# Second half of w_out loaded in a row, down-phase factors split earlier on VectorE, last rows' sums reordered

## The chip, the cores and the metric

One core of a Trainium2 chip runs the kernel. The metric is the device time of one execution in microseconds (us). The engines are TensorE (PE, matrix products, with PEld for its weight loads), VectorE (DVE), ScalarE (ACT), GpSimd (POOL) and SyncE (SP, which here only issues transfers). The 16 DMA engines move data between memory and the chip's buffers.

## The reference, cut to what matters

The input has 1024 rows (T) of 1024 columns (D), in float32.

```python
mod = c_act @ w_ada[l] + b_ada[l]
sh1, sc1, g1, sh2, sc2, g2 = [m[:, None, :] for m in jnp.split(mod, N_MOD, axis=-1)]
h = rmsnorm(x, pre_w_mix[l]) * (1.0 + sc1) + sh1
proj = h @ w_in[l]
# windowed attention -> attn (512 columns); gated linear recurrence -> rec (512 columns)
mix = jnp.concatenate([attn, rec], axis=-1) @ w_out[l]
x = x + g1 * rmsnorm(mix, post_w_mix[l])
h2 = rmsnorm(x, pre_w_mlp[l]) * (1.0 + sc2) + sh2
y = jnp.square(jax.nn.relu(h2 @ w_up[l])) @ w_down[l]       # 4096 hidden columns
x = x + g2 * rmsnorm(y, post_w_mlp[l])
```

## The kernel before

Every large product is made of three matmuls: each operand is split into a rounded high part (a copy on ACT) and a low part (raw minus high, on DVE or POOL), and hi*hi, hi*lo and lo*hi are added in one bank of PE's accumulator (PSUM). A "split" below is this pair of passes over one block of 128 x 512. Names end in r (raw), h and l: `wo_1r` is a raw block of the second half of w_out, `wo_1l` its low part.

The stages follow each other: norm and projections, attention, the recurrence heads (`head_proj`, `head_core`), the out projection, the second norm with its transposes, the up phase and the down phase. Instructions of one engine run in the order in which they are written or placed. A scheduler places them by priority; between `pin(True, ...)` and `pin(False, ...)` the named engines keep the written order, and `tc.issue_after(m)` places what is inside behind the instruction m. SP issues nearly all loads, in one queue.

**Out projection.** w_out is split in two halves of 512 columns with eight row blocks each. `load_wo(half)` loads and splits them; odd blocks have their low part made on POOL, even ones on DVE. The raw blocks pass through a ring of three buffers (`raw_`), so a load waits until the split that used its buffer is done. `op_prep` splits the mixed rows, `op_mm` multiplies, `out_proj` normalises, adds x (loaded as `xr`) and stores: rows of blocks 3 and 7 to the scratch tensor `x1d`, the others to the output itself, onto which the end adds. `cr` are the first blocks of w_up (w_u), `a_2` and `a_3` later blocks of it.

**Second norm and up phase.** `second_raw(th)` transposes half th of the rows (four row blocks) for eight column blocks on PE; behind each ACT and DVE make h and its splits (`bt_1h`, `bt_1l` and so on). `up_cl(f, th)` makes the 24 matmuls of one classical product of the up phase into bank `pu`; `rl` is ACT's relu out of that bank. The rest of the up phase and the whole down phase use a Strassen-Winograd scheme with seven products.

**Down phase.** It runs over (group g, product n). Groups have 4, 4, 3, 3 and 2 hidden blocks, products come in the order 1, 5, 6, 3, 7, 2, 4, and each has four row steps t. `dslot` makes the matmuls of one step, then the step's sum is added by DVE (`acc<-pda`, where pda, pdb, pdc are the banks). The factors (`dw` from the weights, `du` from the up phase) are loaded and split ahead by a queue `seq`: `pump(k)` takes the next k entries and splits each with one ACT and one DVE pass; `target(i)` says how far the queue must be by the end of product i. Gate entries in the same queue sum the row of g2 into `gw2`, and `gate_row` spreads it over the partitions by four matmuls and multiplies.

**Last group and last rows.** The last group is written out as a loop over 24 steps ordered by `order`, with a table `later` of things to do some steps on: `square` (ACT), `root` (DVE and POOL, the power -1/2), `gated` (times gw2), `scaled` (ACT) and `onto_x`, an accumulating store issued by POOL. `last_rows` finishes row blocks 3 and 7 by DVE passes that add x and by plain stores.

Of the kernel before, what the change touches and what calls it, by code (L numbers as in the profile page):

```python
# [47 lines left out]
def hybrid_layer(ctx: ExitStack, tc: tile.TileContext, I, out, dbg=None):  # L48
# [734 lines left out]
    def head_proj(h, th, prev=None, hook=None):  # L783
# [42 lines left out]
        DVE.tensor_tensor(sub4(k4), b4[:, :, :, CH - 1:CH].broadcast_to([P, 4, 4, CH]), b4, ALU.subtract)  # L826
# [98 lines left out]

    def load_wo(half, ks=range(KB)):
        for k in ks:
            wo[half].append(load_split(hT_, f"wo{k}_{half}", I["w_o"][k][:, half * 512:half * 512 + 512],
                                       eng=POOL if k % 2 else DVE))
# [66 lines left out]
    load_wo(0)  # L996
    next(cores[6])
# [51 lines left out]
    x1d = dram.tile([2, P, D], F32, tag="x1d", name="x1d")  # L1049
    xn2 = [None] * TB  # L1050

    def out_proj(tb):
# [14 lines left out]
        for half in range(2):  # L1067
# [5 lines left out]
            nc.gpsimd.dma_start(x1d[tb // 4][:, hs] if tb % 4 == 3 else out[tb * P:(tb + 1) * P, hs], xr)  # L1073
# [22 lines left out]
    def second_raw(th):  # L1096
        for kb in range(KB):
# [212 lines left out]
    def entry_gate(half, k):  # L1310
        def use(raw):
            acc = gw2[:, half * 512:half * 512 + 512]
            if k == 0:
                DVE.tensor_scalar(acc, raw, cs[:, 0:1], None, ALU.mult)
            else:
                DVE.scalar_tensor_tensor(acc, raw, cs[:, k:k + 1], acc, ALU.mult, ALU.add)
        seq.append((f"wada5_{half}_{k}", lambda: I["wada"][5, half, k], use))

    gates = [(half, k) for half in range(2) for k in range(KB)]
    for i, (g, n) in enumerate(stages):  # L1320
# [3 lines left out]
        if 11 <= i and gates:  # L1324
            entry_gate(*gates.pop(0))
        ends.append(len(seq))
    for tb in (3, 7):
        for half in range(2):
            seq.append((f"x1_{tb}_{half}", lambda tb=tb, half=half: x1d[tb // 4][:, half * 512:half * 512 + 512], None))
# [32 lines left out]
    def up_cl(f, th):  # L1362
        pst = mm_ps(f"pu{f}_{th}")
# [8 lines left out]
    for f in range(3):  # L1372
        up_cl(f, 0)
    pin(True, ACT, DVE, POOL)
    second_raw(1)
    pin(False, ACT, DVE, POOL)
    x2ctx.close()
    gw2 = const.tile([P, D], F32, tag="gw1", name="gw2")
    uctx = ExitStack()
# [7 lines left out]
    for f in range(4):  # L1387
        up_cl(f, 1)
# [152 lines left out]
    def target(i):  # L1541

        j = i
        while j + 1 < len(stages) and j + 1 - i <= (2 if i < 14 else 4) and \
                sum(len(GROUPS[stages[m][0]]) for m in range(i, j + 2)) <= 15:
# [5 lines left out]
    def gate_row(t):  # L1551

        hs = [slice(half * 512, half * 512 + 512) for half in range(2)]
        for half in range(2):
            if t == 0:
                hi, lo = split(gw2[:, hs[half]], lambda name, dt: hT_(name, dt), f"g5{half}")
                b5, w5 = hT_(f"b5{half}"), hT_(f"w5{half}")
                nc.gpsimd.dma_start(b5, I["b_g2"][hs[half]].partition_broadcast(P))
                nc.gpsimd.dma_start(w5, I["postw2"][hs[half]].partition_broadcast(P))
                g5[half] = hi, lo, b5, w5  # L1560
            elif t == 2:
                hi, lo, b5, w5 = g5[half]
# [3 lines left out]
            elif t == 3:  # L1566
                DVE.tensor_tensor(gw2[:, hs[half]], g5["p", half], g5[half][2], ALU.add)
                DVE.scalar_tensor_tensor(gw2[:, hs[half]], gw2[:, hs[half]], float(D ** 0.5), g5[half][3], ALU.mult, ALU.mult)
# [9 lines left out]
    for i, (g, n) in enumerate(stages[:28]):  # L1578
        goal = max(prev, target(i))
        for t in range(4):  # L1580
# [7 lines left out]
            want = prev + (goal - prev) * (t + 1) // 4  # L1588
# [3 lines left out]
            if i == 27:  # L1592
# [19 lines left out]
    def gated(tb, half, eng=POOL):  # L1612
        eng.tensor_tensor(accs[tb][half], accs[tb][half], gw2[:, half * 512:half * 512 + 512], ALU.mult)
# [13 lines left out]
    def onto_x(tb):  # L1627

        for half in range(2):
# [4 lines left out]
    order += [(21, 3, 0), (23, 3, 1), (25, 3, 2)]  # L1634
    order.sort()
    bk = {}
    for step, (_, t, k) in enumerate(order):
# [11 lines left out]
        if step < 6:  # L1649
            pump(2)  # L1650
        if k >= 3 and t < 3:
# [4 lines left out]
            else:  # L1656
                on(step + 2, lambda tb=tb: root(tb))
                on(step + 2, lambda tb=tb, half=half: gated(tb, half, DVE))
# [10 lines left out]
    def last_rows():  # L1669
# [5 lines left out]
        gl = [m_(f"gl{half}") for half in range(2)]  # L1675

# [21 lines left out]
        dmm(bx[:, 256:512], g, 4, t, True, slice(256, 512))  # L1698
# [88 lines left out]
```

## Time and profile before

| what | us |
|---|---|
| median of 3 runs | 1112.27 (1111.29, 1113.03, 1112.27) |
| profiled execution | 1115.94 |
| its span in the profile | 1114.2 |
| PE busy | 1082.6 (97%) |
| DVE busy | 811.3 (73%) |
| ACT busy | 592.5 (53%) |
| POOL busy | 394.9 (35%) |
| mean clock of PE in the span | 0.995 |

Times within the profile count from the span's start. The profiled execution took 1.74 us more than its span, and 3.67 us more than the median of the runs, so a sum made from the trace is a difference to be taken off the median, not a time by itself. A matmul is shown busy for longer than the distance to the next, because neighbours overlap in PE. Waits are put down to the instruction that ended them.

### The profile page before, as it was taken

To read this page: it belongs to the slowest core of one execution; us is meant where nothing else is said; L and a number is where in the kernel's file an instruction comes from. 1 tells how busy PE (TensorE), PEld (TensorE's weight loads), DVE (VectorE), ACT (ScalarE), POOL (GpSimd) and SP (SyncE) were. 2 spreads that over 40 slices of the span, in tenths; PEclk is the share of its full clock that TensorE was granted. 3 is DMA by queue.
4 is the path that set the end of the run, shared out by engine and by line. 5 is a ranking of instruction groups with operands and counts; after the bars stand their busy time and mean duration, and the time that the engine had idled before them with its cause. 6 is when DMAs were issued, how large, how long until landed. Compare 5 with 4: busy or idle time off the path is not lost.

```text
span 1114.2 us, 16145 instructions
## 1 busy us (share of the span) xinstructions
PE 1082.6 (97%) x5480; PEld 883.9 (79%) x5480; DVE 811.3 (73%) x1332; ACT 592.5 (53%) x1229; POOL 394.9 (35%) x522
## 2 busy tenths in 40 slices
PE   8899999999999999999999999999999999999995
PEld 7788676778888878888888888888888888888874
DVE  3975877878865673639877767776678787999685
ACT  4645554374565654566655555556565543456334
POOL 2644311034223653422334434444333334300045
PEclk9999999999999999999999999999999999999998
DMA  9701300534410443323577676776899788988546
GB/s 346 257 7 39 133 1 19 194 102 133 134 49 10 130 144 114 112 78 107 199 251 264 222 251 236 250 243 235 274 370 333 269 282 270 335 284 257 165 113 119
DMA packets 101971, 204.16 MB, mean 183 GB/s; under 512 B 13152, under 2 KB 13808, under 8 KB 101888
## 3 DMA queue, kind: packets, MB, share of 16 engines
q1 hardware_dynamic: 86112, 154.78, 40.4%
q0 software_dynamic: 15488, 47.82, 14.3%
q8 instruction: 43, 0.70, 0.3%
q10 hardware_dynamic: 288, 0.52, 0.1%
q14 instruction: 40, 0.33, 0.1%
HBM read 148.03 MB, written 55.05 MB: 182 GB/s over the span
## 4 chain that ended last, share of the span: by engine, by line
PE 77%; DVE 7%; DMA 6%; POOL 3%; ACT 3%; issue 2%; SPq 0%; DVEq 0%; POOLq 0%; ACTq 0%
PE pda L39 13%; PE pua L39 13%; PE pdc L39 7%; PE po L39 7%; PE puc L39 6%; PE pu L39 4%; PE pdb L39 3%; PE pub L39 3%; PE phg L39 3%; PE pv L39 3%; PE phq L39 3%; PE phf L39 2%; PE pq L39 2%; DMA wa<-wada 2%; PE sc L39 1%
## 5 line engine op out<-in xcount | busy, mean ns | idle before, releaser
L39 POOL TENSOR_TENSOR b<-b,b 128x512 f32<-128x512 f32 x64 | 89.5, 1399 | 221.3 <-DMA b<-w_dn 221.0
L39 ACT ACTIVATE s<-s 128x512 f32<-128x512 f32 x84 | 52.9, 631 | 34.0 <-DVE s L39 32.7
L39 ACT ACTIVATE dw<-dwr 128x512 fp32r<-128x512 f32 x72 | 45.3, 629 | 42.4 <-DMA dwr<-td 21.9
L39 DVE TENSOR_TENSOR dw<-dwr,dw 128x512 fp32r<-128x512 f32 x72 | 56.3, 782 | 4.8 <-ACT dw L39 4.8
L39 DVE TENSOR_TENSOR acc<-pda,acc 128x512 f32<-128x512 f32 x68 | 46.1, 682 | 13.5 <-PE pda L39 13.4
L39 POOL DMA_DIRECT2D td<-b x64 | 36.1, 564 | 19.0 <-POOL b L39 19.0
L39 DVE TENSOR_TENSOR wt<-s,wt 128x512 fp32r<-128x512 f32 x42 | 37.1, 884 | 1.4 <-ACT wt L39 1.3
L39 ACT ACTIVATE s<-pua 128x512 f32<-128x512 f32 x28 | 16.7, 596 | 38.2 <-PE pua L39 32.7
L39 ACT ACT_TABLE_LOAD x28 | 35.9, 1283 | 1.2 <-PEq L1780 0.7
L39 POOL DMA_DIRECT2D b<-w_dn x64 | 34.4, 540 | 2.7 <-issue 2.7
L39 DVE TENSOR_TENSOR wt<-a,wt 128x512 fp32r<-128x512 f32 x42 | 34.5, 822 | 0.0
L39 DVE SCALAR_TENSOR_TENSOR macc<-wada,cs,macc 128x512 f32<-128x512 f32 x42 | 32.7, 779 | 2.0 <-DMA wada<-wada 1.3
L39 POOL TENSOR_TENSOR comb<-comb,rd 128x512 f32<-128x512 f32 x8 | 11.7, 1458 | 63.3 <-DVE rd L39 44.2
L39 ACT ACTIVATE wt<-s 128x512 fp32r<-128x512 f32 x42 | 26.3, 627 | 12.3 <-DVE s L39 12.1
L39 PE MATMUL pua<-bt_3h,wt 128*128 128x512 f32 x84 | 32.7, 389 | 0.0
L39 PE MATMUL pua<-bt_0h,wt 128*128 128x512 f32 x84 | 32.7, 389 | 0.0
L39 PE MATMUL pua<-bt_1h,wt 128*128 128x512 f32 x84 | 32.7, 389 | 0.0
L39 PE MATMUL pua<-bt_2h,wt 128*128 128x512 f32 x84 | 32.7, 389 | 0.0
L39 PE MATMUL pda<-dw,du_6h 128*128 128x512 f32 x96 | 29.8, 392 | 1.1 <-DVE acc L39 1.1
L39 DVE TENSOR_TENSOR s<-puc,s 128x512 f32<-128x512 f32 x14 | 9.7, 690 | 28.2 <-issue 27.2
L39 DVE TENSOR_TENSOR acc<-pdc,acc 128x512 f32<-128x512 f32 x36 | 24.5, 682 | 7.5 <-PE pdc L39 7.5
L39 PE MATMUL pdc<-dw,du_3h 128*128 128x512 f32 x96 | 29.7, 390 | 0.2 <-DVE acc L39 0.2
(761 smaller groups left out, 3804.7 us busy)
## 6 DMA issues: line engine op xcount, KB each, us to landing
dur<-ud SPq DMA_DIRECT2D x112, 256.0 KB, 4.2
wada<-wada SPq DMA_DIRECT2D x64, 256.0 KB, 3.5
b<-w_dn POOLq DMA_DIRECT2D x64, 256.0 KB, 5.0
td<-b POOLq DMA_DIRECT2D x64, 256.0 KB, 3.0
dwr<-td SPq DMA_DIRECT2D x64, 256.0 KB, 3.9
a<-w_u SPq DMA_DIRECT2D x56, 256.0 KB, 4.3
dwr<-w_dn SPq DMA_DIRECT2D x48, 256.0 KB, 4.3
ud<-s SPq DMA_DIRECT2D x42, 256.0 KB, 3.6
```

The lines of the kernel that those rows point to most:

```text
L39: ins = op(*args, **kw)
```

## The change

It has five parts. (1) The eight raw blocks of the second half of w_out are loaded in a row on SP, placed behind the last head's instruction `k4`; the first four into tiles of their own, the others into the ring of three. `load_wo(1)` then splits them. (2) The scratch tensor keeps three halves instead of four: half 0 of row block 3 goes to the output, and its final sum is made by an accumulating store of POOL. (3) The second transposes are cut after three of eight blocks, with `up_cl(2, 0)` between, and the third and fourth products of the second half take banks of another pool. (4) In the down phase gate entries start one product earlier, `gw2` starts as b_g2 in its first row (set to zero before), `gate_row` comes one product earlier with two DVE passes for four, `target` reaches six products ahead from product 22 on, and the last group takes four entries of the queue instead of twelve. (5) In the last group all `gated` run on DVE, the three steps of row block t = 3 come behind all others, and the end computes the sum of squares and its root ahead of the second gating and makes three stores instead of four.

```diff
         k4 = g_(f"k4{n}")
-        DVE.tensor_tensor(sub4(k4), b4[:, :, :, CH - 1:CH].broadcast_to([P, 4, 4, CH]), b4, ALU.subtract)
+        marks["k4"] = DVE.tensor_tensor(sub4(k4), b4[:, :, :, CH - 1:CH].broadcast_to([P, 4, 4, CH]), b4, ALU.subtract).ins
...
+    wo_raw = {}
+    def wo_block(half, k):
+        return I["w_o"][k][:, half * 512:half * 512 + 512]
...
         for k in ks:
-            wo[half].append(load_split(hT_, f"wo{k}_{half}", I["w_o"][k][:, half * 512:half * 512 + 512],
-                                       eng=POOL if k % 2 else DVE))
+            wo[half].append(load_split(hT_, f"wo{k}_{half}", wo_block(half, k), eng=POOL if k % 2 else DVE,
+                                       raw=wo_raw.pop((half, k), None)))
...
     load_wo(0)
+    pin(True, SP)
+    with tc.issue_after(marks["k4"]):
+        for k in range(KB):
+            wo_raw[1, k] = load_raw(g_ if k < 4 else raw_, f"wo{k}_1r", wo_block(1, k))
+    pin(False, SP)
...
     X2 = x2ctx.enter_context(tc.tile_pool(name="poolX2", bufs=1))
-    x1d = dram.tile([2, P, D], F32, tag="x1d", name="x1d")
+    x1d = dram.tile([P, 3 * 512], F32, tag="x1d", name="x1d")
+    hold = {(3, 1): slice(0, 512), (7, 0): slice(512, D), (7, 1): slice(D, D + 512)}
...
             DVE.tensor_tensor(xr, xr, t[:, hs], ALU.add)
-            nc.gpsimd.dma_start(x1d[tb // 4][:, hs] if tb % 4 == 3 else out[tb * P:(tb + 1) * P, hs], xr)
+            nc.gpsimd.dma_start(x1d[:, hold[tb, half]] if (tb, half) in hold else out[tb * P:(tb + 1) * P, hs], xr)
...
-    def second_raw(th):
-        for kb in range(KB):
+    def second_raw(th, kbs=range(KB)):
+        for kb in kbs:
...
             acc = gw2[:, half * 512:half * 512 + 512]
-            if k == 0:
-                DVE.tensor_scalar(acc, raw, cs[:, 0:1], None, ALU.mult)
-            else:
-                DVE.scalar_tensor_tensor(acc, raw, cs[:, k:k + 1], acc, ALU.mult, ALU.add)
+            DVE.scalar_tensor_tensor(acc, raw, cs[:, k:k + 1], acc, ALU.mult, ALU.add)
...
             entry_u(p, n)
-        if 11 <= i and gates:
+        if 10 <= i and gates:
...
         ends.append(len(seq))
-    for tb in (3, 7):
-        for half in range(2):
-            seq.append((f"x1_{tb}_{half}", lambda tb=tb, half=half: x1d[tb // 4][:, half * 512:half * 512 + 512], None))
+    for i in range(3):
+        seq.append((f"x1_{i}", lambda i=i: x1d[:, i * 512:i * 512 + 512], None))
...
-    def up_cl(f, th):
-        pst = mm_ps(f"pu{f}_{th}")
+    def up_cl(f, th, mk=mm_ps):
+        pst = mk(f"pu{f}_{th}")
...
         load_cl(f)
-    for f in range(3):
+    for f in range(2):
         up_cl(f, 0)
-    pin(True, ACT, DVE, POOL)
-    second_raw(1)
-    pin(False, ACT, DVE, POOL)
+    pin(True, ACT, DVE, POOL, PE)
+    second_raw(1, range(3))
+    up_cl(2, 0)
+    second_raw(1, range(3, KB))
+    pin(False, ACT, DVE, POOL, PE)
     x2ctx.close()
     gw2 = const.tile([P, D], F32, tag="gw1", name="gw2")
+    POOL.memset(gw2, 0.0)
+    POOL.dma_start(gw2[0:1, :], I["b_g2"].unsqueeze(0))
...
     for f in range(4):
-        up_cl(f, 1)
+        up_cl(f, 1, mm_ps if f < 2 else tp_ps)
...
         j = i
-        while j + 1 < len(stages) and j + 1 - i <= (2 if i < 14 else 4) and \
-                sum(len(GROUPS[stages[m][0]]) for m in range(i, j + 2)) <= 15:
+        while j + 1 < len(stages) and j + 1 - i <= (2 if i < 14 else 4 if i < 22 else 6) and \
+                sum(len(GROUPS[stages[m][0]]) for m in range(i, j + 2)) <= (14 if i in (25, 26) else 15):
...
             if t == 0:
-                hi, lo = split(gw2[:, hs[half]], lambda name, dt: hT_(name, dt), f"g5{half}")
-                b5, w5 = hT_(f"b5{half}"), hT_(f"w5{half}")
-                nc.gpsimd.dma_start(b5, I["b_g2"][hs[half]].partition_broadcast(P))
+                g5["w", half] = w5 = b_(f"w5{half}")
                 nc.gpsimd.dma_start(w5, I["postw2"][hs[half]].partition_broadcast(P))
-                g5[half] = hi, lo, b5, w5
+                g5[half] = split(gw2[:, hs[half]], lambda name, dt: hT_(name, dt), f"g5{half}")
             elif t == 2:
-                hi, lo, b5, w5 = g5[half]
+                hi, lo = g5[half]
...
             elif t == 3:
-                DVE.tensor_tensor(gw2[:, hs[half]], g5["p", half], g5[half][2], ALU.add)
-                DVE.scalar_tensor_tensor(gw2[:, hs[half]], gw2[:, hs[half]], float(D ** 0.5), g5[half][3], ALU.mult, ALU.mult)
+                DVE.scalar_tensor_tensor(gw2[:, hs[half]], g5["p", half], float(D ** 0.5), g5["w", half],
+                                         ALU.mult, ALU.mult)
...
                 pump(2, ends[1])
-            want = prev + (goal - prev) * (t + 1) // 4
+            want = prev + (goal - prev) * (t + 1) // 4 if i < 27 else prev + (goal - prev) * min(t + 1, 3) // 3
...
                 down_sums(LATE[i])
-            if i == 27:
+            if i == 26:
...
-    def gated(tb, half, eng=POOL):
-        eng.tensor_tensor(accs[tb][half], accs[tb][half], gw2[:, half * 512:half * 512 + 512], ALU.mult)
+    def gated(tb, half):
+        DVE.tensor_tensor(accs[tb][half], accs[tb][half], gw2[:, half * 512:half * 512 + 512], ALU.mult)
...
-    def onto_x(tb):
-        for half in range(2):
+    def onto_x(tb, halves=(0, 1)):
+        for half in halves:
...
     order = sorted((7 * t + 2 * k, t, k) for t in range(3) for k in range(7))
-    order += [(21, 3, 0), (23, 3, 1), (25, 3, 2)]
-    order.sort()
+    order += [(27 + k, 3, k) for k in range(3)]
...
             fn()
-        if step < 6:
-            pump(2)
+        if 2 <= step < 6:
+            pump(1)
...
                 on(step + 2, lambda tb=tb: root(tb))
-                on(step + 2, lambda tb=tb, half=half: gated(tb, half, DVE))
+                on(step + 2, lambda tb=tb, half=half: gated(tb, half))
...
         gl = [m_(f"gl{half}") for half in range(2)]
+        ga = m_("ga")
...
         dmm(bx[:, 256:512], g, 4, t, True, slice(256, 512))
+        DVE.tensor_tensor(ga, accs[a][1], gw2[:, h[1]], ALU.mult)
+        for step in sorted(later):
+            rest(step)
...
         sq(accs[b][1], ss[:, 0:1])
+        root(a)
         add(accs[b][0], ba)
-        root(a)
-        gated(a, 1)
+        scaled(a, 0)
+        onto_x(a, (0,))
...
             sq(acp[i], ss[:, 1 + i:2 + i], 256)
-        for step in range(nstep + 3, max(later) + 1):
-            rest(step)
...
         DVE.tensor_scalar(one["part"], ss[:, 0:1], ss[:, 1:2], D * EPS, ALU.add, ALU.add)
-        DVE.tensor_tensor(gl[0], accs[b][0], gw2[:, h[0]], ALU.mult)
...
         POOL.tensor_tensor(one["r"], one["part"], mhalf[:, 0:1], ALU.pow)
-        for tb, rr, src in ((a, rr_[a], accs[a]), (b, one["r"], gl)):
-            for half in range(2):
-                DVE.scalar_tensor_tensor(src[half], src[half], rr[:, 0:1], take(), ALU.mult, ALU.add)
-                (nc.scalar if half else nc.sync).dma_start(out[tb * P:(tb + 1) * P, h[half]], src[half])
+        DVE.tensor_tensor(gl[0], accs[b][0], gw2[:, h[0]], ALU.mult)
+        xa = take()
+        for half in range(2):
+            DVE.scalar_tensor_tensor(gl[half], gl[half], one["r"][:, 0:1], take(), ALU.mult, ALU.add)
+            (nc.scalar if half else nc.sync).dma_start(out[b * P:(b + 1) * P, h[half]], gl[half])
+        DVE.scalar_tensor_tensor(ga, ga, rr_[a][:, 0:1], xa, ALU.mult, ALU.add)
+        nc.sync.dma_start(out[a * P:(a + 1) * P, h[1]], ga)
```

SP, behind the last load of the first half of w_out (one piece of the difference; rows with - stand only before, with + only now; `xr` is x for the residual):

```order
-L39 DMA wo_1r_4169<-w_o 128x512
-L39 DMA wo_1r_4175<-w_o 128x512
-L39 DMA wo_1r_4181<-w_o 128x512
-L39 DMA a_2_5280<-w_u 128x512
-L39 DMA a_2_5286<-w_u 128x512
-L39 DMA a_3_5515<-w_u 128x512
-L39 DMA a_3_5519<-w_u 128x512
-L39 DMA wo_1r_4187<-w_o 128x512
-L39 DMA wo_1r_4219<-w_o 128x512
-L39 DMA wo_1r_4225<-w_o 128x512
+L39 DMA wo_1r<-w_o 128x512 x8
 L39 DMA xr_0_4335<-x 128x512
```

Three loads of the second half stood ahead of four w_up loads, and the rest between and behind; now all eight stand in a row, with those four and the x loads behind them.

DVE, at the start of the last group, before (`du` and `dw` are splits, `acc<-pda_0_10601` and `pdc_0` the last group's first sums):

```order
L39 TENSOR_TENSOR dw_7_10611<-dwr_7_10491,dw_7_10611 128x512
L39 TENSOR_TENSOR du_7l<-dur_7_10507,du_7h 128x512
L39 TENSOR_TENSOR acc_0_7984<-pda_0_10601,acc_0_7984 128x512
L39 TENSOR_TENSOR dw_7_10630<-dwr_7_10523,dw_7_10630 128x512
L39 TENSOR_TENSOR du_7l<-dur_7_10554,du_7h 128x512
L39 TENSOR_TENSOR acc_1_8136<-pdc_0_10620,acc_1_8136 128x512
L39 TENSOR_TENSOR dw_2_10648<-dwr_2_10570,dw_2_10648 128x512
L39 TENSOR_TENSOR du_2l<-dur_2_10591,du_2h 128x512
L39 TENSOR_TENSOR acc_1_8242<-pda_0_10601,acc_1_8242 128x512
L39 TENSOR_TENSOR dw_2_10666<-dwr_2_10609,dw_2_10666 128x512
L39 TENSOR_TENSOR du_2l<-dur_2_10614,du_2h 128x512
```

The same place now (`pda_0_10641` and `pdc_0_10649` are the last group's first banks, `pda_1` to `pda_3` with smaller numbers the product before):

```order
L39 TENSOR_TENSOR acc_0_8698<-pda_1_10103,acc_0_8698 128x512
L39 TENSOR_TENSOR du_2l<-dur_2_10549,du_2h 128x512
L39 TENSOR_TENSOR dw_2_10622<-dwr_2_10567,dw_2_10622 128x512
L39 TENSOR_TENSOR du_2l<-dur_2_10572,du_2h 128x512
L39 TENSOR_TENSOR acc_0_8724<-pda_2_10125,acc_0_8724 128x512
L39 TENSOR_TENSOR acc_0_8751<-pda_3_10147,acc_0_8751 128x512
L39 TENSOR_TENSOR acc_0_7986<-pda_0_10641,acc_0_7986 128x512
L39 TENSOR_TENSOR acc_1_8138<-pdc_0_10649,acc_1_8138 128x512
L39 TENSOR_TENSOR dw_4_10666<-dwr_4_10588,dw_4_10666 128x512
L39 TENSOR_TENSOR acc_1_8244<-pda_0_10641,acc_1_8244 128x512
L39 TENSOR_TENSOR du_4l<-dur_4_10593,du_4h 128x512
L39 TENSOR_TENSOR acc_1_8244<-pdc_0_10649,acc_1_8244 128x512
```

The splits of products 7 and 2 stood between the last group's sums, two per sum, and now stand ahead of them; one split per sum is left, of product 4.

DVE at the end, before (`gl` is the gating of row block 7, `l_part` and `ssf` parts of the sums of squares, the last rows add x):

```order
L39 TENSOR_TENSOR gl_10923<-acc_1_8216,gw_5263 128x512
L39 TENSOR_SCALAR l_part<-ssl 128x1
L39 TENSOR_TENSOR gl_10922<-acc_0_8749,gw_5263 128x512
L39 TENSOR_TENSOR l_part<-l_part,ssl 128x1
L39 SCALAR_TENSOR_TENSOR acc_0_8109<-acc_0_8109,rrf_10981,x_3_0_10664 128x512
L39 SCALAR_TENSOR_TENSOR acc_1_8336<-acc_1_8336,rrf_10981,x_3_1_10669 128x512
L39 SCALAR_TENSOR_TENSOR gl_10922<-gl_10922,l_r,x_7_0_10686 128x512
L39 SCALAR_TENSOR_TENSOR gl_10923<-gl_10923,l_r,x_7_1_10691 128x512
```

The end now (`ga` is the gating of half 1 of row block 3):

```order
L39 TENSOR_TENSOR ga<-acc_1_8338,gw_5263 128x512
L39 TENSOR_TENSOR acc_1_8218<-pda_3_10883,acc_1_8218 128x512
L39 TENSOR_SCALAR ssf_10977<-ssf_10948 128x1
L39 TENSOR_TENSOR acc_0_8751<-pda_3_10883,acc_0_8751 128x512
L39 TENSOR_TENSOR acc_0_8751<-pdlx,acc_0_8751 128x256 x2
L39 TENSOR_TENSOR gl_10930<-acc_1_8218,gw_5263 128x512
L39 TENSOR_SCALAR l_part<-ssl 128x1
L39 TENSOR_TENSOR l_part<-l_part,ssl 128x1
L39 TENSOR_TENSOR gl_10929<-acc_0_8751,gw_5263 128x512
L39 SCALAR_TENSOR_TENSOR gl_10929<-gl_10929,l_r,x_1_10625 128x512
L39 SCALAR_TENSOR_TENSOR gl_10930<-gl_10930,l_r,x_2_10664 128x512
L39 SCALAR_TENSOR_TENSOR ga<-ga,rrf_10978,x_0_10620 128x512
```

The second gating moved behind the two parts of the sum, and of four passes that add x three are left, of which that of row block 3 is now last.

## The prediction, made before the changed kernel was run

> **What bounds the kernel now.** I read the page first, then the table of stretches, then the waits of PE in the stretches where PE is not full, and last the instructions around each wait.
>
> ```profile
> span 1114.2 us, 16145 instructions
> ...
> PE 1082.6 (97%) x5480; PEld 883.9 (79%) x5480; DVE 811.3 (73%) x1332; ACT 592.5 (53%) x1229; POOL 394.9 (35%) x522
> ...
> PE 77%; DVE 7%; DMA 6%; POOL 3%; ACT 3%; issue 2%; SPq 0%; DVEq 0%; POOLq 0%; ACTq 0%
> ```
>
> The span has 31.6 us without a running matmul. The change adds and removes no matmul of weight, so it can only earn from those 31.6 us, and only where its edits lie. The table of stretches (length, then busy us of PE, PEld, DVE, ACT and POOL; granted clock; DMA share and GB/s) says how much there is in each place:
>
> ```profile
> 387.00:402.00 15.00, 12.91 (x57) 9.25 (x57) 12.63 (x25) 9.54 (x36) 7.78 (x7) 1.00 0.56 178
> ...
> 491.00:510.00 19.00, 18.27 (x95) 14.59 (x94) 13.13 (x17) 14.20 (x24) 6.41 (x5) 1.00 0.20 76
> 510.00:1049.00 539.00, 538.54 (x2377) 445.60 (x2376) 422.64 (x593) 292.74 (x500) 182.88 (x221) 1.00 0.76 259
> 1049.00:1057.60 8.60, 8.60 (x40) 7.12 (x39) 6.84 (x11) 3.95 (x8) 0.00 (x0) 1.00 0.40 124
> 1057.60:1065.00 7.40, 6.39 (x27) 4.71 (x26) 7.33 (x13) 1.31 (x3) 0.00 (x0) 1.00 0.47 146
> 1065.00:1075.00 10.00, 9.44 (x40) 7.17 (x39) 8.66 (x14) 4.06 (x9) 2.22 (x2) 1.00 0.39 128
> 1075.00:1086.00 11.00, 10.63 (x47) 8.47 (x46) 7.57 (x14) 5.54 (x14) 8.77 (x10) 1.00 0.56 77
> ...
> 1101.00:1114.20 13.20, 0.00 (x0) 0.00 (x0) 6.12 (x10) 2.30 (x8) 4.55 (x6) 0.59 0.62 140
> ```
>
> From 510 to 1049 PE is full (538.54 of 539.00 us): there nothing can be won and much lost. A product of the fourth group of the down phase is 36 matmuls (four row blocks of nine), and 539.00/2377 = 0.227 us each makes 8.16 us. The last row counts 13.2 us after the last matmul. In the other four places PE's waits are these, in the order of the table:
>
> ```profile
> PE po L39 <- POOL wo_1l L39: 1.5, 2, 0.8
> PE po L39 <- DVE wo_1l L39: 0.4, 1, 0.4
> PE po L39 <- ACT wo_1h L39: 0.2, 1, 0.2
> ...
> PE pu L39 <- POOL bt_1l L39: 0.5, 1, 0.5
> PE pu L39 <- ACT rl L39: 0.2, 1, 0.2
> ...
> PE pda L39 <- DVE acc L39: 1.7, 4, 0.8
> PE pdc L39 <- DVE acc L39: 0.2, 1, 0.2
> ...
> L39 PE MATMUL pda<-dw,du_6h 128*128 128x512 f32 x96 | 29.8, 392 | 1.1 <-DVE acc L39 1.1
> ```
>
> A stall costs more than its wait: a matmul is shown busy for 0.39 us but the next could have started 0.227 us after it, so each adds 0.16 us. The stalls are thus worth A (out projection) 2.1 + 4 x 0.16 = 2.7 us; B (start of the up phase) 0.7 + 2 x 0.16 = 1.0 us; D (start of the last group) 1.9 + 5 x 0.16 = 2.7 us.
>
> **A, the second half of w_out.** The wait ends with the low part of a weight block, and behind that stands a late load:
>
> ```profile
> 387.21 1.53 SPq L39 DMA_DIRECT2D wo_1r<-w_o  x3
> 388.78 0.90 SPq L39 DMA_DIRECT2D xr<-x  x2
> 392.31 5.18 SPq L39 DMA_DIRECT2D wo_1r<-w_o  x2
> ...
> 397.16 2.63 DMA wo_1r<-w_o
> ...
> 400.50 0.50 PE L39 MATMUL po<-wo_1h,mxh 128*128 128x512 f32 x1 [0.16 <-ACT wo_1h L39]
> 401.85 0.50 PE L39 MATMUL po<-wo_1l,mxh 128*128 128x512 f32 x1 [0.85 <-POOL wo_1l L39]
> ...
> L39 ACT ACTIVATE wo_1h<-wo_1r x8: 617/632/647, 381.2 to 399.8; 128x512 fp32r<-128x512 f32 x8
> L39 POOL TENSOR_TENSOR wo_1l<-wo_1r,wo_1h x4: 1271/1312/1345, 383.5 to 400.5; 128x512 fp32r<-128x512 f32 x4
> ...
> DMA to landing us min/median/max: 2.5/2.9/3.5
> ...
> 389.20 1.03 POOL L39 TENSOR_TENSOR r_h<-t_h,mhalf 128x4 f32<-128x4 f32 x1
> 390.26 0.69 DVE L39 TENSOR_TENSOR on<-o,r_h 128x512 f32<-128x512 f32 x1 [0.91 <-POOL r_h L39]
> ```
>
> The new order issues all eight loads in a row behind the last load of the first half, four into their own tiles, so these four come by about 381, and their splits too. But the other four go through a ring of three buffers, so the eighth waits until the fifth's split on DVE is done. Costed: the fourth block's low part now stands ahead of r_h on POOL (1.31 us), so r_h ends near 391.2 instead of 390.23, `on` near 391.9, the fifth split near 392.6; the eighth load is issued there, lands 2.6 to 3.5 later (395.2 to 396.1), ACT rounds it (0.63), POOL subtracts (1.31): ready at 397.1 to 398.1. PE, without its stalls, asks for it near 398.9 (401.85 less 3.0: the 2.7 and the short waits ahead of it). The margin is 0.8 to 1.8 us, small but positive. Gain 2.7; ends: 1.2 if the last stall stays, 3.0 with the short waits. What is moved past: four w_u loads and the loads of x for the residual (xr, cr) now stand behind the eight on SP, and start at 392.6 at the earliest, where xr's began at 388.78 before; they are used after 402, so they cost nothing as long as the eighth leaves before about 398.
>
> **B, transposes cut in two.** Before, the fourth half's products began right behind the transposes and met bt_1l (POOL, 1.31 us). With up_cl(2,0) put after three transposed blocks, 24 matmuls (24 x 0.227 = 5.4 us) cover the copies and splits of the first three, and the products f >= 2 take banks from another pool, so the bank wait on `rl` goes. Gain 1.0; ends 0.3 (a bt_1l still late) and 1.0. The memset of gw2 and its small load on POOL are new: POOL is busy 6.41 of 19 us in this stretch, which hides one such pass; if it stood ahead of bt_1l it would cost at most two 128x512 passes, 2.6 us, less the cover of 5.4: zero.
>
> **C, the rows of x1 and the gate.** One store goes to the output instead of a scratch buffer, and one load of the end falls away: 0. Gating starts one product earlier: the DVE work is the same, in a stretch where DVE is busy 422.64 of 539.00 us and PE does not wait: 0, with an end of -0.6 (one DVE pass).
>
> **D, splits six products ahead.** At the start of the last group two splits per step (one for the weight, one for u) stand on DVE ahead of each accumulation, and PE waits for the bank:
>
> ```profile
> 1059.60 0.68 DVE L39 TENSOR_TENSOR acc<-pda,acc 128x512 f32<-128x512 f32 x1
> ...
> 1060.80 0.68 DVE L39 TENSOR_TENSOR du_7l<-dur,du_7h 128x512 fp32r<-128x512 f32 x1
> ...
> 1079.92 1.97 POOL L39 TENSOR_TENSOR acc<-acc,gw 128x512 f32<-128x512 f32 x1
> ```
>
> The distance between two DVE passes is 1.2/2 = 0.60 us. In this place DVE is busy 7.33 of 7.40 us: it is the bound. The change moves eight of the twelve splits of the last group to the two products ahead of it, and makes the gate's row one product earlier, with two passes for four. These two then hold for DVE 8 accumulations, 16 splits and 4 passes of the gate's row (two splits of it and the two gates), 28 x 0.60 = 16.8 us, in 2 x 8.16 us and the gate's 4 matmuls (0.9), 17.2 us: just full, where it was 6.84 of 8.60. The last group's first step then meets no queue, and one of its steps (6 matmuls, 1.36 us) holds one split and one or two accumulations, 1.2 to 1.8 us, where the first six held two splits and as many accumulations, 1.8 to 2.4 us. Gating on DVE adds seven passes of 0.60 us over the last group, where DVE has 11.00 - 7.57 = 3.4 us free in 11 us, and takes seven of 1.97 us off POOL. I leave 0.5 us for two short waits where a gate pass stands ahead of an accumulation. Gain 2.7 - 0.5 = 2.2; ends: 0.3 (DVE a full pass behind at each of four steps) and 2.7.
>
> **E, the end.**
>
> ```profile
> 1101.54 1.58 POOL L39 TENSOR_TENSOR acc<-acc,gw 128x512 f32<-128x512 f32 x1
> ...
> 1101.67 2.01 DVE L39 TENSOR_TENSOR gl<-acc,gw 128x512 f32<-128x512 f32 x1
> ...
> 1104.33 0.15 DVE L39 TENSOR_TENSOR l_part<-l_part,ssl 128x1 f32<-128x1 f32 x1
> ...
> 1104.56 1.00 POOL L39 TENSOR_TENSOR l_r<-l_part,mhalf 128x1 f32<-128x1 f32 x1
> 1105.72 1.40 DVE L39 SCALAR_TENSOR_TENSOR gl<-gl,l_r,x 128x512 f32<-128x512 f32 x2
> ...
> 1107.15 0.34 ACTq L1717 DMA_DIRECT2D out<-gl  x1
> ...
> DMA to landing us min/median/max: 3.9/4.5/6.7
> ```
>
> The DVE pass `gl` took 2.01 us instead of 0.68 beside a POOL pass; the change takes POOL's pass away (1.3 us less) and puts the sum ahead of the second gating, so the sum is held only by ACT's squares, to which one scaling is added (about 0.6). I take the root 1.0 us earlier. Behind it stand three passes (2.0 us) instead of two with two of another row before (1.40), so the last store goes 0.4 to 0.5 us earlier, with the same landing of 4.5. The accumulating store of row 3 goes out before, near 1102.5, and even with 6.7 lands by 1109.2, ahead of the last. Gain 0.5; ends -0.3 and 1.0. [...]
>
> **The sum.** 2.7 + 1.0 + 0 + 2.2 + 0.5 = 6.4 us, less 0.1 for C. The profiled execution took 1115.94 us (span 1114.2 and 1.74 around it), 3.67 over the median of 1112.27, so the same work would be profiled at 1109.6; on the median, 1112.27 - 6.3 = 1106.0 us.
>
> **The rivals.**
> *The eighth load is still late* (it is not one go: it waits for a buffer). For it: margin of 0.8 us at a landing of 3.5, and four engines' turns before it; against: landings here were mostly 2.5 to 2.9. A then earns 1.2: 1107.5.
> *DVE becomes the bound of the last sixty us.* For it: 16.8 us of DVE in 17.2, and seven gate passes more; against: DVE's rows there hold 3.4 us free in the following 11. D then earns 0.3 and the end nothing: 1112.27 - 2.7 - 1.0 - 0.3 + 0.1 = 1108.4; with A also half lost, 1109.9.
> *Slower: the queue of SP stands behind the eighth load.* Its buffer is freed by DVE, which waits for `on`, which waits for POOL's root, behind a split that itself waits for a load: a ring over four engines, with the x loads of the out projection behind it on SP. To be slower by 0.2%, A must turn from +2.7 to -5.9: PE would stand until 398.9 + 8.6 = 407.5 for the last block. The row of `on` (0.91 us of waiting) puts this far off. If it slipped by 9 us: 1115.
>
> **How the numbers follow.** About 0.2% (2.2 us) is what a measurement tells from no change. Forecast (all four stalls go) 0.60; eighth load late 0.15; DVE the bound 0.15, of which a third with other losses ends within 0.2%; slower by SP's queue or another bank wait 0.04; the change does nothing that counts 0.06. Range: the forecast's own is 1104.7 (all upper ends: 3.0 + 1.0 + 2.7 + 1.0 = 7.7 less 0.1) to 1107; with the two rivals it reaches 1109.5, and below I allow 0.7 more: 1104.0 to 1109.5. Faster: 0.60 + 0.15 + 0.10 = 0.85; same 0.05 + 0.06 = 0.11; slower 0.04.
>
> **What the profile after would show.** A: the first four wo_1r loads near 380, the eighth near 392.6, no wait of PE on wo_1l. B: no wait on bt_1l at the transposes. D: no PE wait on DVE acc near 1060 (there six us earlier), and DVE near full in the two products ahead of it. E: `gl` at 0.68 us and three stores on SP and ACT. I am wrong if PE's waits on acc reappear ahead of or inside the last group with the same sum, or if the eighth load goes after 394.

## The result, and the profile after

The changed kernel takes 1106.87 us (median of 6 runs, 1105.48 to 1107.51) against 1112.33 us before (6 runs, 1111.29 to 1114.78): a ratio of 0.9946, 95% interval 0.9934 to 0.9959, that is 4.6 to 7.3 us faster. Forecast were 1106.0 us, 1104.0 to 1109.5.

The page of the changed kernel, its head and the chain by engine:

```profile
span 1103.7 us, 16146 instructions
...
PE 1078.3 (98%) x5480; PEld 883.3 (80%) x5480; DVE 817.4 (74%) x1337; ACT 596.3 (54%) x1230; POOL 393.5 (36%) x515
...
PE 83%; DVE 7%; ACT 3%; POOL 2%; issue 2%; DMA 1%; SPq 0%; POOLq 0%; DVEq 0%; ACTq 0%
```

In the chain, DMA falls from 6% to 1%. The span is 10.5 us shorter, more than the runs say, and not all of it is the change: the 200th matmul, in the first stage, already starts at 36.17 instead of 38.62 us, and the kernels of the experiments stand there between 36.0 and 38.0, whatever they changed. So 2.4 us belong to that one execution of before. Six matmuls near its start (`spare`) took 2.75 us where the changed kernel needed 1.64 (before, then now); what slowed them is not known:

```profile
8.74 2.75 PE L39 MATMUL spare<-spare,ones_r 128*128 128x512 f32 x6
...
7.28 1.64 PE L39 MATMUL spare<-spare,ones_r 128*128 128x512 f32 x6
```

A further 0.75 us, at 789 us, was a single long split on DVE, which no other trace has in that place. The rest is read from the starts of the same matmuls in both traces.

The stretches of the changed kernel (from 1034.40 the two products ahead of the last group; the last row begins at the last matmul's end):

```profile
384.60:399.60 15.00, 14.97 (x71) 12.07 (x70) 12.15 (x24) 11.50 (x43) 10.24 (x9) 1.00 0.41 132
479.00:498.00 19.00, 18.32 (x97) 15.19 (x96) 10.99 (x12) 11.44 (x19) 7.74 (x7) 1.00 0.16 58
...
1034.40:1051.60 17.20, 17.20 (x77) 14.25 (x76) 16.91 (x28) 7.70 (x13) 0.00 (x0) 1.00 0.69 218
...
1042.00:1051.00 9.00, 9.00 (x42) 7.44 (x41) 9.00 (x16) 4.52 (x8) 0.00 (x0) 1.00 0.80 249
1051.00:1058.40 7.40, 7.40 (x34) 6.13 (x33) 5.15 (x8) 0.42 (x1) 0.00 (x0) 1.00 0.24 87
...
1078.80:1092.90 14.10, 12.15 (x57) 9.43 (x55) 10.51 (x21) 8.13 (x19) 9.53 (x12) 1.00 0.89 114
1092.90:1103.70 10.80, 0.00 (x0) 0.00 (x0) 4.75 (x10) 2.14 (x7) 2.31 (x3) 0.71 0.64 144
```

The out projection is full (14.97 of 15.00, was 12.91), and so is the start of the last group (7.40 of 7.40, was 6.39). DVE makes 28 passes in the two products ahead of it and is busy 16.91 of 17.20 us there, as the sum of 28 passes had said, with 9.00 of 9.00 us in the last part. But PE now idles 2 us in the last 14, where it idled half a microsecond before:

```profile
1086.00:1101.00 15.00, 14.48 (x69) 11.72 (x67) 10.63 (x19) 9.31 (x22) 11.25 (x13) 1.00 0.72 102
```

The end behind the last matmul is 10.8 instead of 13.6 us. The waits of PE that are left, at the start of the up phase and in the last group:

```profile
PE pu L39 <- POOL bt_1l L39: 0.7, 1, 0.7
...
PE pda L39 <- DVE acc L39: 1.9, 2, 1.2
```

By starts of the same matmuls the parts are worth: the out projection 3.2 us (the lead, by which a matmul starts earlier than before, grows from 2.31 to 5.55), the start of the up phase 0.6 (to 6.12), the start of the last group 3.0, less 2.2 given back in its last steps, and the end 2.75. These parts add up to 7.3 us and come from one execution of each kernel; the medians of the runs differ by 5.5, so the parts together are nearly 2 us too much for a usual execution, and which of them is too large is not known. That the last steps lose most of what the end earns is the part of this that I had not seen.

### The profile page after: what moved, and what is told of

Read it like the earlier page. It is cut to its first block, busy times and chain, and to the rows that moved or that the text cites. A ratio compares the mean times of both kernels' runs of the same rounds, so it can differ in the third digit from the quotient of the medians.

```text
span 1103.7 us, 16146 instructions
## 1 busy us (share of the span) xinstructions
PE 1078.3 (98%) x5480; PEld 883.3 (80%) x5480; DVE 817.4 (74%) x1337; ACT 596.3 (54%) x1230; POOL 393.5 (36%) x515
## 4 chain that ended last, share of the span: by engine, by line
PE 83%; DVE 7%; ACT 3%; POOL 2%; issue 2%; DMA 1%; SPq 0%; POOLq 0%; DVEq 0%; ACTq 0%
PE pda L39 14%; PE pua L39 14%; PE po L39 8%; PE pdc L39 7%; PE puc L39 7%; PE pu L39 4%; PE pub L39 3%; PE pdb L39 3%; PE phg L39 3%; PE pv L39 3%; PE phq L39 3%; PE pq L39 2%; PE phf L39 2%; PE pk L39 1%; PE sc L39 1%
## 5 line engine op out<-in xcount | busy, mean ns | idle before, releaser
L39 DVE TENSOR_TENSOR dw<-dwr,dw 128x512 fp32r<-128x512 f32 x72 | 53.0, 737 | 5.9 <-ACT dw L39 5.9
L39 POOL TENSOR_TENSOR rrf<-ssf,mhalf 128x1 f32<-128x1 f32 x7 | 7.5, 1073 | 109.9 <-DVE ssf L39 109.8
L39 PE MATMUL pda<-dw,du_7h 128*128 128x512 f32 x96 | 29.6, 389 | 0.0
```

The costliest lines, as they stand in the source:

```text
L39: ins = op(*args, **kw)
```

## The experiments

All ratios are to the kernel before, run on the same chip, with their 95% intervals; one of 0.001 is 1.1 us.

**The loads alone.**

```diff
-            wo[half].append(load_split(hT_, f"wo{k}_{half}", I["w_o"][k][:, half * 512:half * 512 + 512],
-                                       eng=POOL if k % 2 else DVE))
+            wo[half].append(load_split(hT_, f"wo{k}_{half}", wo_block(half, k), eng=POOL if k % 2 else DVE,
+                                       raw=wo_raw.pop((half, k), None)))
...
+            wo_raw[1, k] = load_raw(g_ if k < 4 else raw_, f"wo{k}_1r", wo_block(1, k))
```

> The kernel before with the loads of the second half of w_out alone in a row, four into their own tiles. Theory (A is the largest part): the stalls of PE on wo_1l go, 3.0 us less, ratio 0.9973, and nothing is given back behind. Rival (out projection waits for the x loads that now stand behind the eighth load on SP): the stalls move to PE's or DVE's work behind 400, ratio 0.999 or more.

1109.70 us, ratio 0.9971 (0.9961 to 0.9981): 3.2 us. PE waits nowhere on wo_1l, and the lead over the kernel before goes from 1.88 us ahead of the out projection to 5.12 behind it and stays there. The theory stands; the x loads behind the eighth cost nothing.

**The place on SP without the own tiles.**

```diff
-            wo_raw[1, k] = load_raw(g_ if k < 4 else raw_, f"wo{k}_1r", wo_block(1, k))
+            wo_raw[1, k] = load_raw(raw_, f"wo{k}_1r", wo_block(1, k))
```

> The changed kernel with all eight loads of the second half in a row on SP but all through the ring of three buffers. Theory (it is the four own tiles that bring the loads forward, not the place on SP; load k waits for the split of load k-3): the loads spread out again over 375 to 397, PE waits for wo_1l as before (2.5 to 3.5 us), 1109.5 to 1110.5. Rival (the place in the queue is what counts, ahead of the w_up loads): stalls of 1 us or less, 1107 to 1108.

1109.75 us, ratio 0.9971 (0.9960 to 0.9982). The rows of the tile and the waits of PE in this run:

```profile
L39 SPq DMA_DIRECT2D wo_1r<-w_o x8: 327/328/383, 376.0 to 394.7; - x8
...
PE po L39 <- POOL wo_1l L39: 1.5, 2, 0.9
PE po L39 <- ACT wo_1h L39: 0.5, 1, 0.5
PE po L39 <- DVE wo_1l L39: 0.2, 1, 0.2
```

In the changed kernel the loads go from 365.2 to 390.8 and none of these waits is there; before, they went from 378.3 to 397.2 (changed kernel, then before):

```profile
L39 SPq DMA_DIRECT2D wo_1r<-w_o x8: 327/404/433, 365.2 to 390.8; - x8
...
L39 SPq DMA_DIRECT2D wo_1r<-w_o x8: 327/328/382, 378.3 to 397.2; - x8
```

So the new place in the queue does nothing without the four tiles. With the ring alone the loads stand 2.3 to 2.5 us earlier than before, which is this trace's lead from the first stage, and all the stalls are back (3.2 us by starts). Whether the four tiles alone would do it at the old place on SP was not run.

**The down phase alone** (lookahead, gate row, four entries in the last group).

```diff
-        while j + 1 < len(stages) and j + 1 - i <= (2 if i < 14 else 4) and \
+        while j + 1 < len(stages) and j + 1 - i <= (2 if i < 14 else 4 if i < 22 else 6) and \
...
-            if i == 27:
+            if i == 26:
...
-        if step < 6:
-            pump(2)
+        if 2 <= step < 6:
+            pump(1)
```

> The kernel before with the down-phase part alone (lookahead of six, the gate's row one product earlier, four entries in the last group instead of twelve); the gating on POOL, the order of the last group and the end as before. Theory (splits taken out of the last group free DVE for its sums): the five waits of PE on DVE acc between 1060 and 1087 go, 2.5 to 3.0 us, so 1109.3 to 1109.8 against 1112.3, a ratio near 0.9975. Rival (DVE is the bound of the last sixty us, the queue only moves): waits on acc of the same sum appear in the two products ahead of the last group, and the time stays at 1112 (ratio 0.9995 to 1.000).

1108.52 us, ratio 0.9964 (0.9951 to 0.9976): 4.0 us, more than expected. PE waits on no sum in the whole last group; the trace gains 3.7 us up to the last matmul. DVE, nearly full in the two products ahead, is not the bound.

**The last rows alone.**

```diff
-    order += [(21, 3, 0), (23, 3, 1), (25, 3, 2)]
-    order.sort()
+    order += [(27 + k, 3, k) for k in range(3)]
...
-    def gated(tb, half, eng=POOL):
-        eng.tensor_tensor(accs[tb][half], accs[tb][half], gw2[:, half * 512:half * 512 + 512], ALU.mult)
+    def gated(tb, half):
+        DVE.tensor_tensor(accs[tb][half], accs[tb][half], gw2[:, half * 512:half * 512 + 512], ALU.mult)
...
+        scaled(a, 0)
+        onto_x(a, (0,))
```

> The kernel before with the last rows' part alone (t = 3 steps behind all others, gating on DVE, three stores, row block 3's half 0 through an accumulating store); its last group still takes twelve entries of the queue. Theory: behind the last matmul the end gets about 2.7 us shorter (13.6 to some 10.9), because the last store is issued 1.0 us earlier and lands in about 2.7 instead of 4.5 us when no accumulating store is in flight beside it; against that stand two new waits of PE on acc in the last steps, some 2 us, and the waits at the start of the group stay, so 1111 to 1112 in all (ratio 0.999 to 1.000). Rival (the shorter landing in the profile after was chance, the last steps cost nothing): landing 4.5 us, the end only 1 us shorter, and 1111.3.

1113.73 us, ratio 1.0005 (0.9995 to 1.0014). The end is 11.0 us behind the last matmul, and the last matmul is 3.0 us later: PE waits 5.0 us on DVE's sums where it waited 1.9. What the end gains the last steps lose, as expected, but by more: the time lies above the 1111 to 1112 us that were expected.

```profile
PE pda L39 <- DVE acc L39: 4.8, 5, 1.3
PE pdc L39 <- DVE acc L39: 0.2, 1, 0.2
```

**All but the last rows** (loads, transposes and down phase as changed, end as before).

```diff
-    order += [(27 + k, 3, k) for k in range(3)]
+    order += [(21, 3, 0), (23, 3, 1), (25, 3, 2)]
+    order.sort()
...
-    def gated(tb, half):
-        DVE.tensor_tensor(accs[tb][half], accs[tb][half], gw2[:, half * 512:half * 512 + 512], ALU.mult)
+    def gated(tb, half, eng=POOL):
+        eng.tensor_tensor(accs[tb][half], accs[tb][half], gw2[:, half * 512:half * 512 + 512], ALU.mult)
...
-        scaled(a, 0)
-        onto_x(a, (0,))
```

> The changed kernel without its last-rows part: the order of steps, the gating on POOL and the four stores are those of before; loads, transposes and down-phase lookahead as changed. Theory (the last-rows part earns nothing, what it takes off the end it loses in the last steps): 0.5 to 1.2 us faster than the changed kernel, ratio to before 0.9925 to 0.994. Rival (the parts do add, the last rows are worth 1 to 2 us): ratio 0.996.

1105.91 us, ratio 0.9938 (0.9925 to 0.9952), against 0.9946 of the changed kernel. The intervals overlap: that the last-rows part costs something, as expected, is not shown by the times, only that it earns nothing that can be measured.

**Why PE waits in the last steps.** In the changed kernel the chain of the last group reads:

```profile
1075.57 0.95 POOL rrf L39
...
1077.17 0.24 ACT acc L39
...
1077.78 0.71 ACT fin L39 x2
...
1078.60 0.21 DVE ssf L39
1078.81 2.41 DVE acc L39 x4
...
1081.67 0.71 ACT acc L39
1082.38 0.62 ACT fin L39 x2
...
1083.02 0.78 DVE acc L39 x2
...
1084.23 0.20 DVE ssf L39
1084.43 1.21 DVE acc L39 x2
...
1085.69 1.65 PE pda L39 x6
```

POOL's root releases ACT's scaling (`acc`), behind it on ACT stands a square (`fin`), on which DVE's next pass waits, and behind that pass stands the sum that frees PE's bank. Five runs take this apart, and the end with it. First the gating that is not beside a root back to POOL:

```diff
-    def gated(tb, half):
+    def gated(tb, half, eng=DVE):
...
-                on(step + 2, lambda tb=tb, half=half: gated(tb, half))
+                on(step + 2, lambda tb=tb, half=half: gated(tb, half, POOL))
             else:
```

> The changed kernel with the early gatings of the last group (those not beside a root) back on POOL, as before; all else as changed. Theory (PE waits in the last steps because the t = 3 steps stand close together behind sums that wait, in DVE's order, for a sum of squares of ACT): the root's first pass on DVE waits for ACT as well, so one of the two stalls (0.9 and 1.4 us) stays: 1105.5 to 1106.9 against 1106.9. Rival (the gating on DVE alone is the cause): both stalls go, 1104.7 (ratio to the kernel before 0.993).

1107.44 us, ratio 0.9948 (0.9936 to 0.9960). The rival fell: both stalls stayed, 0.5 and 2.2 us by starts, where the theory had one go. Ahead of the second, in this run, POOL and DVE gate side by side:

```profile
1083.07 1.89 POOL L39 TENSOR_TENSOR acc<-acc,gw 128x512 f32<-128x512 f32 x1
...
1083.20 2.32 DVE L39 TENSOR_TENSOR acc<-acc,gw 128x512 f32<-128x512 f32 x1
```

DVE's pass, 0.68 us at 1078.40 without a gating on POOL beside it, took 2.32 beside POOL's, and the sum that PE waits for stands behind it. At the end of the kernel before, `gl` took 2.01 us beside POOL's gating of 1.58; in the changed kernel, where POOL gates nothing, it takes 0.68. So this run tells only that moving the gating back does not help: it puts another wait in the place of the one it takes.

Then the old order of steps:

```diff
-    order += [(27 + k, 3, k) for k in range(3)]
+    order += [(21, 3, 0), (23, 3, 1), (25, 3, 2)]
+    order.sort()
```

> The changed kernel with the old order of steps in the last group (the three first steps of t = 3 between those of t = 2, not behind them); gating stays on DVE. Theory (the close order is the cause): both stalls of the last steps go, about 2 us, and the end behind the last matmul stays at 10.9: 1104.9 (ratio to before 0.9933). Rival (gating on DVE is the cause): the stalls stay and the time with them, 1106.9; or the end grows again since row block 2 is finished later, by up to 1 us.

1107.37 us, ratio 0.9954 (0.9942 to 0.9967): a miss in the time. Both stalls went, and the last matmul came 2.0 us sooner, but the end grew to 14.6 us. The t = 3 steps behind all others earn their stalls back: under them row blocks 2 and 6 are finished and stored. ACT's squares stood behind its scalings here too (1086.65, then 1087.90), so that order alone makes no stall either.

Next, with the old order, the root of row block 3 ahead of two stores on POOL, and its scaling and store behind the last root:

```diff
+        root(a)
         for step in sorted(later):
             rest(step)
         add(accs[b][1], ba)
         sq(accs[b][1], ss[:, 0:1])
-        root(a)
         add(accs[b][0], ba)
-        scaled(a, 0)
-        onto_x(a, (0,))
...
         POOL.tensor_tensor(one["r"], one["part"], mhalf[:, 0:1], ALU.pow)
+        scaled(a, 0)
+        onto_x(a, (0,))
```

> The changed kernel with the old order of steps (no stalls) and, at the end, row block 3's root ahead of row block 6's stores on POOL and its scaling and store behind the last root. Theory (in the run with the old order the end grew to 14.6 us since the root of row block 3 stood on POOL behind two stores that wait for ACT, and ACT's last squares behind the scaling that waits for this root): the end shrinks to about 12.3 us, PE has no stall in the last steps, ratio to before 0.992 to 0.994, some 0.7 us under the changed kernel. Rival (the end grows because the t = 3 steps come earlier and row blocks 2 and 6 are finished behind them, whatever the order on POOL): the end stays above 14 us and the ratio at 0.995.

1107.84 us, ratio 0.9956 (0.9944 to 0.9968): a miss again, with a new cause. The last store was issued 2.7 us sooner (1097.5, was 1100.2), but the end was 15.3 us, since the stores landed late. The landing times of the last five stores, two of them accumulating:

```profile
DMA to landing us min/median/max: 5.1/5.4/6.6
```

So the same kernel without the last accumulating store:

```diff
         scaled(a, 0)
-        onto_x(a, (0,))
```

> The kernel of e7 without the last accumulating store (half 0 of row block 3 is scaled but not added to the output). Theory (the last plain stores land late, 5 to 6 us after issue in e7, because an accumulating store issued just before is in flight on the same DMA engines): they land 2.5 to 3.3 us after issue and the end shrinks from 15.3 to about 12.5 us behind the last matmul. Rival (they are late for another reason, such as row block 6's stores or the time itself): 4.5 us or more.

This kernel leaves half 0 of row block 3 without its last part. A single run: 1104.08 us, the end 12.0 us behind the last matmul. The three plain stores at the end:

```profile
DMA to landing us min/median/max: 2.7/2.7/2.7
```

They need 2.7 us here, and 5.1 to 5.9 in the run above, behind an accumulating store issued 0.9 to 2.2 us before them. In that run the first plain store landed at 1102.14, right behind the accumulating one at 1101.97; so it was before (1110.20 behind 1110.03), where they took 4.5 to 5.0. This is what the changed kernel's end lives on (2.6 to 3.2, with the accumulating store issued 2.7 us before the first of them): the span ends 5.3 us behind the issue of its last store, 7.0 before.

Two things stay open. The store that was left out is an accumulating one and one that POOL issues, and no run tells these two apart. And the end does not follow the landing all the way: in the five traces that end as the changed kernel does, the last store lands 2.0 to 3.0 us after its issue, and the end is 10.8 us in all of them.

Last, the ring itself: the changed kernel with the scaling one step later, so that squares stand ahead of it on ACT.

```diff
-                    on(step + 3, lambda tb=tb, hf=hf: scaled(tb, hf))
-                on(step + 4, lambda tb=tb: onto_x(tb))
+                    on(step + 4, lambda tb=tb, hf=hf: scaled(tb, hf))
+                on(step + 5, lambda tb=tb: onto_x(tb))
```

> The changed kernel with the scaling of each finished row block (ACT) and its stores one step later in the last group, so that the sums of squares of the next rows stand ahead of the scaling on ACT; the order of PE's steps and all passes of DVE stay. Theory (a ring: DVE's root and gating wait for a square on ACT, which stands behind a scaling that waits for the root on POOL, which waits for DVE; behind DVE's wait stands the sum that frees PE's bank): both stalls of the last steps (0.9 and 1.4 us) go, the end stays between 10.8 and 11.8 us behind the last matmul, 1.2 to 2.2 us under the changed kernel, ratio to before 0.9926 to 0.9936. Rival (the close t = 3 steps on one bank are enough, whatever ACT's order): the stalls stay, ratio 0.9946.

1103.12 us (4 runs, 1102.83 to 1103.67), ratio 0.9912 (0.9898 to 0.9925): faster than the changed kernel by more than I expected. No wait of PE on a sum is left in the last group, and the end is 10.8 us. Where the changed kernel's ACT squared behind scaling (1076.54, then 1077.78), here:

```profile
1076.59 0.60 ACT L39 ACTIVATE fin<-acc 128x512 f32<-128x512 f32 x1 [2.00 <-DVE acc L39]
1077.12 0.19 ACT L39 ACTIVATION_READ_ACCUMULATOR fin<-acc 128x1 f32 x1
1077.21 1.32 ACT L39 ACTIVATE acc<-acc,rrf 128x512 f32<-128x512 f32 x2
...
1077.77 0.20 DVE L39 TENSOR_SCALAR ssf<-ssf 128x1 f32<-128x1 f32 x1
```

The square waits only for its sum, and DVE's root pass follows without a wait. DVE has the same passes in the same order, and PE its steps: the ring is shown, and the gating on DVE and the close steps are no cause by themselves. The stall needs the close steps and ACT's order together; without either it goes.

The edit also moves POOL's stores one step later, and these are part of the second stall: in the changed kernel a store held POOL until 1079.96, while the root behind it was ready at 1078.81. How much of that stall the stores make and how much ACT's order was not separated. The first stall has no store in its way. Of the 3.8 us between the two ratios the trace shows 2.2 (by starts, up to the last matmul); the rest lies within the two intervals.

**What is left at the start of the up phase**, on top of the last kernel:

```diff
-    second_raw(1, range(3))
+    second_raw(1, range(5))
     up_cl(2, 0)
-    second_raw(1, range(3, KB))
+    second_raw(1, range(5, KB))
```

> The kernel of e9 with five of the eight transposed blocks ahead of the 24 covering matmuls instead of three. Theory (what is left at the start of the up phase, 0.83 us on bt_1l, comes from ACT, which idles 2.3 us under the cover because only three blocks are there to copy): the wait on bt_1l goes, 0.8 us less than e9, ratio 0.992 to 0.993. Rival (the bound is elsewhere: DVE's or POOL's own splits of the last blocks): the wait stays at 0.5 us or more.

1103.63 us, ratio 0.9913 (0.9900 to 0.9927): not to be told from the kernel above. In the trace the wait on bt_1l is gone, and the stretch gains 1.3 instead of 0.65 us, but that is below what the times can show. ACT sat idle 1.2 us under the cover instead of 2.3, as the theory had it.

## Why the prediction was right

The time, the range and the sign held. Of the sum's terms, A, B and C came within 0.5 us, and D and E were wrong by 1.4 and 2.2 us, in opposite directions: that these two offset each other is luck. The bounds were also drawn a little tight by the prediction's own working: its two rivals together gave 1109.9 us, and the range ended at 1109.5.

**A** was put at 2.7 and is 3.2 us, by the trace and by the loads alone. The working by steps held: the eighth load was forecast for 392.6 and went at 390.8, with the out projection 2.3 us ahead in that trace. The first rival (the eighth late) and the one on the other side (SP's queue) fell with it.

**B** was put at 1.0 and is 0.6. The bank wait went, but one wait on bt_1l stayed (0.84 us by starts, 0.66 before). The step that failed is that the 24 matmuls cover enough: they cover the copies and splits of the first three blocks, and ACT then idles, while the other five blocks come as late as before.

**C** at about 0 held.

**D** was put at 2.2 and is 0.8 (3.0 less 2.2). The splits were worth 3.0 at the group's start and 4.0 alone (0.9964), so the rival of DVE as the bound fell, although it was full. The step that failed is "I leave 0.5 us for two short waits where a gate pass stands ahead of an accumulation": there were two, as said, of 0.9 and 1.4 us by starts. The place was right and the cause not: the gate passes cost DVE's time only; it is what they and the roots wait for, ACT's squares behind a scaling, that made them long. I had counted passes, not the order of the queue that they wait on. The prediction also gave the move of the t = 3 steps behind all others no term at all, and in these runs the stalls come only with it: with the old order both went, while the end grew to 14.6 us.

**E** was put at 0.5 and is 2.75. That "the last store goes 0.4 to 0.5 us earlier, with the same landing of 4.5" did not hold: measured from the last matmul's end it went 1.0 us earlier, since the root came 1.5 us earlier where 1.0 was taken, and the landing fell to 2.6, by which the span ends 1.7 us sooner behind that store. The row for the landing was taken from an end where the last accumulating store was issued 1.9 us before the first plain one (1103.3 and 1105.2), and the change put 2.7 us between the two (1094.4 and 1097.1). `gl` at 0.68 us came as forecast. The last root took 0.94 us, and 1.00 before. Where POOL has nothing else in hand, a root beside a DVE pass that reads a PSUM bank (`acc<-pda`) takes 0.55 to 0.56 us in the seven traces that show one (the changed kernel and six of the experiments), and a root that starts beside a gating on DVE takes 0.93 to 0.95, as the last root did. The 1.00 of before stood beside two DVE passes that add x (1.40 us at 1104.39). So the gating that now starts beside the last root made it no longer than it was before. In the last steps one root took 1.68 us: POOL was still issuing a store until 1079.96, and by then the next gating had begun on DVE (1079.92).

```profile
1079.33 1.68 POOL L39 TENSOR_TENSOR rrf<-ssf,mhalf 128x1 f32<-128x1 f32 x1
...
1092.82 0.56 POOL L39 TENSOR_TENSOR rrf<-ssf,mhalf 128x1 f32<-128x1 f32 x1 [2.11 <-DVE ssf L39]
...
1095.36 0.94 POOL L39 TENSOR_TENSOR l_r<-l_part,mhalf 128x1 f32<-128x1 f32 x1
```

## What to carry to other kernels

Where several engines finish rows in a chain, count for each pass what it waits for and what stands ahead of that on its own queue: here two lines, which put squares ahead of scalings on ACT and stores a step later, were worth more than the whole reordering of the end. The loads that pass through a ring came no sooner for standing sooner in the queue; with four buffers of their own besides, they did. And the plain stores that end this kernel landed late, 4.5 to 5.9 us after their issue, in two traces (before, and with row block 3's root first) where an accumulating store of POOL went out 1.9 and 0.9 us before the first of them, and 2.6 to 3.2 us after it in the changed kernel, where that store went out 2.7 us before: take a landing time from a row together with the stores issued around it.

## What the runs showed of the hardware

A gap in PE's work of 2.46 us between two starts (in the run with early gatings on POOL) was followed by a stretch at a lower granted clock. Gaps of 1.6 and 1.7 us in the last steps of the changed kernel and of the run with the last rows alone were not (granted clock 1.00 behind both), nor was a gap of 2.0 us that the kernel before has at 53.2 us and the changed kernel at 50.7 (1.00 behind both). The stretches of that run:

```profile
1083.90:1086.20 2.30, 0.23 (x2) 0.03 (x1) 2.30 (x4) 0.24 (x1) 2.02 (x2) 1.00 1.03 156
1086.20:1091.00 4.80, 4.80 (x14) 3.83 (x15) 2.51 (x5) 2.42 (x4) 4.34 (x5) 0.66 0.63 85
```

The granted clock is 0.66 for 4.8 us, and seven matmuls there start 0.43 us apart instead of 0.227, so this stall cost some 1.4 us more than its length. This was seen in one execution, and no run shows what sets the clock.
